# Combination stage of a hybrid Conformer/SSD layer: order of its buffers, queue of its tile loads, places of the norm's two mean products

## The chip, the cores and the metric

The kernel runs on one core of a Trainium2 chip. The core has five engines with a queue of their own each: TensorE (PE, matrix products; PEld is its weight load), VectorE (DVE), ScalarE (ACT), GpSimd (POOL) and SyncE (SP, which here only issues DMAs). An engine takes the instructions of its queue strictly in order; engines wait for one another on semaphores. Data lies in HBM; it is moved by DMA to SBUF (128 partitions) and PE writes its results to PSUM. The metric is device time in microseconds (us) of one execution, the median of several.

## What is computed

One layer over x of shape (1, 1024, 1024), all in float32: a layer norm, a token mixer with two branches, an output projection with a residual and a norm, and a convolutional gated feed-forward block. The stage that matters here joins the two branches; the layer norm of the first one goes over the 1024 channels, its convolution has 31 taps, and `ssd_branch` ends in a product from 2048 to 1024 channels:

```python
def conformer_branch(u_glu, dw_w, dw_b, ln_g, ln_b, w_out):
    a, g = jnp.split(u_glu, 2, axis=-1)
    v = a * jax.nn.sigmoid(g)
    v = causal_dwconv(v, dw_w, dw_b)
    v = jax.nn.silu(layer_norm(v, ln_g, ln_b))
    return v @ w_out

def reference(...):
    h = layer_norm(x, ln_in_g, ln_in_b)
    ...
        y_a = conformer_branch(u_glu, ...)
        y_b = ssd_branch(z, xbc, dt_raw, ...)
        mix = (jax.nn.sigmoid(gate_a) * y_a + jax.nn.sigmoid(gate_b) * y_b) @ w_o[l]
        h = layer_norm(DN_ALPHA * h + mix, ln1_g[l], ln1_b[l])
```

## The kernel before

**Tiling and stages.** The 1024 positions are worked off in two halves of 512 (hh = 0 and 1). Activations are held with channels on partitions: a 1024-channel activation is 8 tiles of 128 x 512. For each half come `mixers` (input projections, both convolutions, the SSD recurrence), `combine` (the stage changed here) and an output projection; the feed-forward block follows for all positions. A float32 product is made of three products of rounded parts, high x high, high x low and low x high (lines 170, 171, 172, in `mm3`), so `project`, one 128-column slice of a weight times 1024 channels, is 24 instructions on PE. `weights` loads a slice by SP (L145), rounds it on ACT (L147) and takes the low part on DVE (L151).

**The order of the queues.** Program order is not queue order. The framework's scheduler simulates the engines with its own durations and gives each engine, among the instructions that it holds ready, the one of highest priority. Priority is program order; `tc.high_priority(offset=n)` moves instructions n places ahead (a negative n, behind). What comes out is a fixed order for each queue; on the chip an instruction also waits for its own semaphores.

**Memory.** `mixers` and `combine` each open a pool at the same place of SBUF, one after the other. Within a pool the buffers lie in the order in which their tags first appear. `reuse_waits="tile"` means that a tile of the later pool waits on the chip only for the users of earlier tiles on its own bytes. In `mixers` the order is, in KB per partition: rstd 2, m 4, cbm 0.5, u 3 x 2, xbc 4 x 2, x4 2 x 8, zs 2 x 8, v 4 x 2.1, then smaller ones up to 84. `zs` is read last by L562, `x4` by L602 (the low parts of yT), `v` by the convolution's taps.

**The 31-tap convolution.** `conv31` runs on DVE, 30 instructions L453 for each of 8 channel tiles, two tiles at a time; it has a priority 1500 places behind, so that it fills DVE's gaps. The results of tiles 0 to 5 are stored to `c_scr` (L463); the last two (6 and 7, the dictionary `accs`) stay in SBUF.

**`combine` before.** For j in 0..7: `gate()` is a `project` of a weight gb with hT and a sigmoid on ACT (L669); the y part stored by the mixer is loaded by SP (L677); a `project` of a weight sp with yT (called sp0 to sp7 below, the gates gb0 to gb7); DVE adds and multiplies (L681, L682) into `mb` j. The gates run one ahead: gb0, gb1, sp0, gb2, sp1, and so on. Behind the loop stands the convolution's norm, raised by 900 places: SP loads the six stored tiles (L692), POOL adds the eight tiles (L697, L699), PE multiplies with a matrix of 1/1024 (**L701, the first mean product**, which gives every partition the mean over channels), DVE subtracts (L704), ACT squares (L706, L709), POOL adds the squares (L710), PE multiplies again (**L712, the second mean product**, the variance), ACT and DVE make the reciprocal root (L713, L714), and each tile is scaled (L717), goes through SiLU (L718) and is split into high and low part, sT (L186, L187). Then come eight projects co0 to co7 of the convolution's output weight with sT. In the first half `ln_in_second` reuses the buffers of this norm to make the input norm of the second half: gain and shift come into `stats` and `sq` (L276), x into `c0` to `c3` (L279).

PSUM has four banks for projects (tag `acc`) and four for the rest (tag `sm`); a project needs a free bank.

Of the kernel before, what the change touches and what calls it, by code (L numbers as in the profile page):

```python
# [8 lines left out]
F32 = mybir.dt.float32  # L9
F32R = mybir.dt.float32r  # L10
AF = mybir.ActivationFunctionType
# [5 lines left out]
P = 128  # L17
D = 1024
T = 1024
HALF = 512  # L20
# [30 lines left out]
CT_A, CT_G, CT_X, CT_B, CT_C, CT_GA, CT_GB, CT_Z = 0, 8, 16, 32, 36, 40, 48, 56  # L51
# [4 lines left out]
def kernel(  # L56
# [31 lines left out]
    def bank(which):  # L88
        n_ps[0] += 1
        pl, tag = (pacc, "acc") if which else (psm, "sm")  # L90
        return pl.tile([P, 512], F32, tag=tag, name=f"{tag}{n_ps[0]}")
# [17 lines left out]
        out=quads, in_=ident.rearrange("p (j h) -> p h j", j=4), axis=AX.X, op=ALU.add  # L109
# [23 lines left out]
    c_scr = [dram.tile([8, P, HALF], F32, name=f"c_scr{i}") for i in range(2)]  # L133
# [6 lines left out]
    y_scr = [dram.tile([8, P, HALF], F32, name=f"y_scr{i}") for i in range(2)]  # L140

    def weights(src, name, keep=None, kept=None):
        with tc.high_priority(offset=4000):
            st = wst.tile([P, D], F32, tag="st", name=f"st_{name}")
            SY.dma_start(st, src)  # L145
            w = wsp.tile([P, 2, D], F32R, tag="w", name=f"w_{name}")
            A.copy(w[:, 0, :], st)  # L147
            if kept is not None:
                SY.dma_start(w[:, 1, :].bitcast(F32), kept)
            else:  # L150
                V.tensor_tensor(  # L151
                    out=w[:, 1, :], in0=st, in1=w[:, 0, :].bitcast(F32), op=ALU.subtract
                )
            if keep is not None:
                SY.dma_start(keep, w[:, 1, :].bitcast(F32))
        return w
# [7 lines left out]
    def big_tile(name):  # L164
        return big.tile([P, 2, KD, HALF], F32R, tag="big", name=name)

    def mm3(ps, wa, xa, start, stop, more=False):


        TE.matmul(ps, wa(0), xa(0), start=start, stop=False, skip_group_check=more)  # L170
        TE.matmul(ps, wa(0), xa(1), start=False, stop=False, skip_group_check=more)  # L171
        TE.matmul(ps, wa(1), xa(0), start=False, stop=stop, skip_group_check=more)  # L172

    def project(ps, w, xs):
        for k in range(KD):
            mm3(
                ps,
                lambda i: w[:, i, k * P : (k + 1) * P],
                lambda i: xs[:, i, k, :],
                k == 0,  # L180
                k == KD - 1,
            )

    def split_to(dst, j, src):

        A.copy(dst[:, 0, j, :], src)  # L186
        V.tensor_tensor(  # L187
            out=dst[:, 1, j, :], in0=src, in1=dst[:, 0, j, :].bitcast(F32), op=ALU.subtract
        )
# [40 lines left out]
    def ln_apply(t, mv, rs, i, g, b):  # L230
        V.scalar_tensor_tensor(
            out=t, in0=t, scalar=mv[:, i, 0:1], in1=g, op0=ALU.subtract, op1=ALU.mult
        )
        V.scalar_tensor_tensor(
            out=t, in0=t, scalar=rs[:, i : i + 1], in1=b, op0=ALU.mult, op1=ALU.add
        )
# [29 lines left out]
                    transpose_to(hT, xt, t, 0, KD)  # L266
        return hT

    def ln_in_second(pl):

        hT = big_tile("hT1")
        gb = [pl.tile([P, D], F32, tag=tag, name=f"in1_{tag}") for tag in ("stats", "sq")]
        for i in range(2):
            G.dma_start(gb[i], gin[i])  # L276
        for t in range(4):
            xt = pl.tile([P, D], F32, tag=f"c{t}", name=f"x1_{t}")
            G.dma_start(xt, x[HALF + t * P : HALF + (t + 1) * P, :])  # L279
# [379 lines left out]
    def combine(hh, hT, yT, accs):  # L659

        with pool(f"comb{hh}") as pl:
            mb, gbs = [], []

            def gate():
                j = len(gbs)
                pg = bank(1)
                project(pg, weights(wcol[CT_GB + j], f"gb{hh}_{j}"), hT)
                gb = pl.tile([P, HALF], F32, tag="gate", bufs=3, name=f"gb{hh}_{j}")
                A.activation(out=gb, in_=pg, func=AF.Sigmoid)  # L669
                gbs.append(gb)  # L670

            gate()
            for j in range(8):
                if j < 7:
                    gate()
                ya = pl.tile([P, HALF], F32, tag="yb", bufs=2, name=f"yb{hh}_{j}")
                SY.dma_start(ya, y_scr[hh][j])  # L677
                ps = bank(1)
                project(ps, weights(wssm[j, 1], f"sp{hh}_{j}"), yT)
                m = pl.tile([P, HALF], F32, tag=f"mb{j}", name=f"mb{hh}_{j}")  # L680
                V.tensor_add(m, ya, ps)  # L681
                V.tensor_mul(m, m, gbs[j])  # L682
                mb.append(m)
            with tc.high_priority(offset=900):
                cs = []
                for i in range(8):
                    if i in accs:
                        cs.append(accs[i])
                        continue
                    if i % 2 == 0:  # L690
                        pair = pl.tile([P, 2, HALF], F32, tag=f"c{i // 2}", name=f"cc{hh}_{i}")
                    SY.dma_start(pair[:, i % 2, :], c_scr[hh][i])  # L692
                    cs.append(pair[:, i % 2, :])
                stats = pl.tile([P, 2, HALF], F32, tag="stats", name=f"stats{hh}")
                squares = pl.tile([P, 2, HALF], F32, tag="sq", name=f"csq{hh}")
                mean = stats[:, 0, :]
                G.tensor_add(mean, cs[0], cs[1])  # L697
                for c in cs[2:]:
                    G.tensor_add(mean, mean, c)  # L699
                pm = bank(0)  # L700
                TE.matmul(pm, mean_w, mean, start=True, stop=True)  # L701
                var = stats[:, 1, :]
                for i, c in enumerate(cs):
                    V.tensor_tensor(out=c, in0=c, in1=pm, op=ALU.subtract)  # L704
                    if i == 0:
                        A.activation(out=var, in_=c, func=AF.Square)  # L706
                    else:
                        sq = squares[:, i % 2, :]
                        A.activation(out=sq, in_=c, func=AF.Square)  # L709
                        G.tensor_add(var, var, sq)  # L710
                pv = bank(0)
                TE.matmul(pv, mean_w, var, start=True, stop=True)  # L712
                A.activation(out=var, in_=pv, func=AF.Sqrt, bias=eps)  # L713
                V.reciprocal(out=var, in_=var)  # L714
                sT = pl.tile([P, 2, KD, HALF], F32R, tag="sT", name=f"sT{hh}")
                for i, c in enumerate(cs):
                    V.tensor_mul(c, c, var)  # L717
                    A.activation(  # L718
                        out=c,
                        in_=c,  # L720
                        func=AF.Silu,
                        scale=pc[:, PC_LG + i : PC_LG + i + 1],
                        bias=pc[:, PC_LB + i : PC_LB + i + 1],
                    )
                    split_to(sT, i, c)
            mixT = big_tile(f"mixT{hh}")
# [439 lines left out]
    yT, accs = mixers(1, hT)  # L1166
    mixT, _ = combine(1, hT, yT, accs)
# [122 lines left out]
```

## Time and profile before

| | us |
|---|---|
| median of 3 runs | 1971.43 (1966.43 to 1974.03) |
| the profiled execution | 1972.21 |
| its span, first to last instruction | 1970.1 |
| PE busy | 1932.9 (98%) |
| DVE busy | 1600.7 (81%) |
| ACT busy | 1083.8 (55%) |
| POOL busy | 203.1 (10%) |

The page has the busy time of each engine, the chain of work that ended last, and groups of instructions. Views of the trace used below: the waits of PE (which line waited for which), timelines of one engine (start, duration, line, operation, output tile <- input tiles, count, and in brackets the idle time before it and what ended it), groups for one tile or one line (count, shortest/median/longest in ns, first and last start in us) and busy times in chosen windows. Consecutive like instructions are merged into one row with a count.

### The profile page before, as it was taken

Reading aid. Unit: us, or ns where it says so; the run is one execution under the profiler, and the core shown is the slowest. Engines: PE = TensorE matmul, PEld = TensorE weight load, DVE = VectorE, ACT = ScalarE, POOL = GpSimd, SP = SyncE. Lnnn points to the kernel's source line nnn. Section 1 sums busy time; section 2 is a strip of 40 time slices with the busy share of each in tenths; the row PEclk is TensorE's granted clock in tenths of the full one; section 3 lists DMA queues with packets and bytes.
Section 4 is the critical chain, followed back from the end, with each engine's and each line's share of the span. In section 5 each row is a group of like instructions: output and inputs, shape, how many; then the busy total and the mean of one; then the engine's idle time right before and its main releaser. Section 6 shows DMA issues by size and latency. Waiting matters only on the chain.

```text
span 1970.1 us, 25840 instructions
## 1 busy us (share of the span) xinstructions
PE 1932.9 (98%) x9453; PEld 1575.2 (80%) x9453; DVE 1600.7 (81%) x2224; ACT 1083.8 (55%) x1617; POOL 203.1 (10%) x246
## 2 busy tenths in 40 slices
PE   9999999999899999999999999999999999999997
PEld 8888777777688788888778888888888888878886
DVE  7599999999786547898999655587788888879778
ACT  4676767653263265868775435365555555544432
POOL 0001010110310000110101040001000000121010
PEclk9999999999999999999999999999999999999999
DMA  7645455546455665555554644576455555588673
GB/s 270 221 171 198 161 206 177 166 162 202 157 187 176 215 221 182 190 184 198 178 178 148 213 162 129 169 255 227 160 166 183 175 185 184 179 293 297 201 230 125
DMA packets 128416, 378.36 MB, mean 192 GB/s; under 512 B 15104, under 2 KB 15648, under 8 KB 128288
## 3 DMA queue, kind: packets, MB, share of 16 engines
q1 hardware_dynamic: 109152, 321.63, 48.7%
q0 software_dynamic: 12800, 43.54, 6.4%
q10 hardware_dynamic: 6336, 11.54, 1.6%
q8 instruction: 74, 1.21, 0.3%
q14 instruction: 54, 0.44, 0.1%
HBM read 289.99 MB, written 86.65 MB: 191 GB/s over the span
## 4 chain that ended last, share of the span: by engine, by line
PE 71%; DVE 16%; issue 5%; DMA 5%; ACT 2%; POOL 1%; SPq 0%; DVEq 0%; ACTq 0%; POOLq 0%
PE acc L172 16%; PE acc L171 16%; PE acc L170 16%; PE sm L171 6%; PE sm L172 6%; PE sm L170 6%; DVE c L453 5%; DVE w_c L151 1%; DVE x L408 1%; DMA rstd<-nrm_scr 1%; PE sm L536 1%; DMA dr<-wdown 1%; PE sm L539 1%; DVE x L588 1%; DMA b_scr<-fo 1%
## 5 line engine op out<-in xcount | busy, mean ns | idle before, releaser
L170 PE MATMUL acc<-hT,w_c 128*128 128x512 f32 x1000 | 391.8, 392 | 0.5 <-ACT x L406 0.5
L171 PE MATMUL acc<-hT,w_c 128*128 128x512 f32 x1000 | 390.7, 391 | 0.0
L172 PE MATMUL acc<-hT,w_c 128*128 128x512 f32 x1000 | 390.1, 391 | 0.6 <-DVE w_c L151 0.5
L453 DVE SCALAR_TENSOR_TENSOR c<-v,pc,c 128x512 f32<-128x512 f32 x480 | 370.6, 798 | 7.3 <-ACT c L442 4.7
L170 PEld LDWEIGHTS acc<-hT,w_c 128*128 128x128 f32 x1000 | 187.8, 188 | 41.7 <-issue 1.9
L172 PEld LDWEIGHTS acc<-hT,w_c 128*128 128x128 f32 x1000 | 187.8, 188 | 41.2 <-DVE w_c L151 1.4
L171 PEld LDWEIGHTS acc<-hT,w_c 128*128 128x128 f32 x1000 | 187.8, 188 | 39.2 <-issue 1.1
L147 ACT CAST w_c<-st_c 128x1024 fp32r<-128x1024 f32 x128 | 133.8, 1045 | 108.5 <-PE acc L172 90.0
L515 POOL TENSOR_TENSOR ce<-ce,xbc 128x1024 f32<-128x1024 f32 x28 | 74.1, 2648 | 694.3 <-ACT ce L514 694.3
L1077 ACT CAST w_dn<-dr 128x1024 fp32r<-128x1024 f32 (+1 forms) x73 | 68.8, 944 | 87.5 <-DMA dr<-wdown 25.3
L504 ACT ACTIVATE m<-ab,acs 128x128 f32<-128x128 f32 x256 | 78.4, 390 | 48.2 <-PE sm L536 47.0
L170 PE MATMUL sm<-h1s,w_s 128*128 128x512 f32 x264 | 102.7, 389 | 0.0
L171 PE MATMUL sm<-h1s,w_s 128*128 128x512 f32 x264 | 102.7, 389 | 0.0
L172 PE MATMUL sm<-h1s,w_s 128*128 128x512 f32 x264 | 102.2, 389 | 0.0
L151 DVE TENSOR_TENSOR w_c<-st_c,w_c 128x1024 fp32r<-128x1024 f32 x64 | 79.1, 1239 | 22.3 <-ACT w_c L147 22.1
L1078 DVE TENSOR_TENSOR w_dn<-dr,w_dn 128x1024 fp32r<-128x1024 f32 (+1 forms) x73 | 78.7, 1089 | 5.3 <-ACT w_dn L1077 5.3
L408 DVE SCALAR_TENSOR_TENSOR x<-u,pc,x 128x512 f32<-128x512 f32 x96 | 76.7, 810 | 5.7 <-ACT x L406 5.7
L172 PE MATMUL acc<-h1b,w_ue 128*128 128x512 f32 x176 | 68.9, 395 | 1.5 <-DVE w_ue L151 1.5
L170 PE MATMUL acc<-h1b,w_ue 128*128 128x512 f32 x176 | 68.8, 391 | 0.0
L171 PE MATMUL acc<-h1b,w_ue 128*128 128x512 f32 x176 | 68.6, 390 | 0.0
L170 PE MATMUL sm<-h1b,w_s 128*128 128x512 f32 x176 | 68.5, 389 | 0.0
L171 PE MATMUL sm<-h1b,w_s 128*128 128x512 f32 x176 | 68.5, 389 | 0.0
(324 smaller groups left out, 4542.3 us busy)
## 6 DMA issues: line engine op xcount, KB each, us to landing
st_c<-wcol SPq DMA_DIRECT2D x128, 512.0 KB, 4.4
low_scr<-w_c SPq DMA_DIRECT2D x64, 512.0 KB, 2.9
w_c<-low_scr SPq DMA_DIRECT2D x64, 512.0 KB, 4.4
ab<-acs_scr SPq DMA_DIRECT2D x32, 512.0 KB, 4.1
dr<-wdown SPq DMA_DIRECT2D x55, 256.0 KB, 4.8
st_wo<-wo SPq DMA_DIRECT2D x24, 512.0 KB, 4.0
st_ue<-wup SPq DMA_DIRECT2D x22, 512.0 KB, 4.2
first_scr<-first ACTq DMA_DIRECT2D x44, 256.0 KB, 2.9
```

The costliest lines, as they stand in the source:

```text
L147: A.copy(w[:, 0, :], st)
L151: V.tensor_tensor(out=w[:, 1, :], in0=st, in1=w[:, 0, :].bitcast(F32), op=ALU.subtract)
L170: TE.matmul(ps, wa(0), xa(0), start=start, stop=False, skip_group_check=more)
L171: TE.matmul(ps, wa(0), xa(1), start=False, stop=False, skip_group_check=more)
L172: TE.matmul(ps, wa(1), xa(0), start=False, stop=stop, skip_group_check=more)
L408: V.scalar_tensor_tensor(out=o, in0=u[:, k : k + HALF], scalar=pc[:, wc + k : wc + k + 1], in1=o, op0=ALU.mult, op1=ALU.add,)
L453: V.scalar_tensor_tensor(out=accs[i], in0=v[:, k : k + HALF], scalar=pc[:, wc + k : wc + k + 1], in1=accs[i], op0=ALU.mult, op1=ALU.add,)
L504: A.activation(out=m[:, h, :], in_=ab[:, h, :], func=AF.Relu, scale=-1.0, bias=acs[:, c, 8 * g + h : 8 * g + h + 1],)
L515: G.tensor_tensor(out=ce, in0=ce, in1=CT[:, cs].unsqueeze(1).to_broadcast([P, 8, P]), op=ALU.mult)
L536: TE.matmul(o, xs[:, h * HP : (h + 1) * HP], m[:, h, :], start=True, stop=first)
L1077: A.copy(w[:, 0, cs], src)
L1078: V.tensor_tensor(out=w[:, 1, cs], in0=src, in1=w[:, 0, cs].bitcast(F32), op=ALU.subtract)
```

## The change

The buffers of `combine` are named in another order: `sq` and `stats` first, then (as they come) `gate` and `yb`, then all eight `mb`, then in the first half the x tile `c3`, then `c0` to `c2`, and `sT` last. Inside j = 0, behind the y load, `early_tiles` allocates them and loads the six stored tiles by POOL's queue, raised by 5000 places; the additions of the mean stand there too, no longer raised. `deviations` (L701 to L710 of before) stands behind j = 2 in the first half and j = 1 in the second, `normed` (L712 to the splits) behind j = 4 and j = 3; before, both stood behind j = 7 and were raised by 900. `ln_in_second` takes the `c3` tile made earlier. No arithmetic is added or removed.

```diff
-    def ln_in_second(pl):
+    def ln_in_second(pl, x3):
...
-            xt = pl.tile([P, D], F32, tag=f"c{t}", name=f"x1_{t}")
+            xt = x3 if t == 3 else pl.tile([P, D], F32, tag=f"c{t}", name=f"x1_{t}")
...
+            gbs = []
+            squares = pl.tile([P, 2, HALF], F32, tag="sq", name=f"csq{hh}")
+            stats = pl.tile([P, 2, HALF], F32, tag="stats", name=f"stats{hh}")
+            late, cs = [], []
+            mean, var = stats[:, 0, :], stats[:, 1, :]
+
+            def early_tiles():
+                mb = [pl.tile([P, HALF], F32, tag=f"mb{j}", name=f"mb{hh}_{j}") for j in range(8)]
+                late.extend(
+                    pl.tile([P, D], F32, tag="c3", name=f"x1_{t}") for t in (3,) if not hh
+                )
+                pairs = [
+                    pl.tile([P, 2, HALF], F32, tag=f"c{i}", name=f"cc{hh}_{i}") for i in range(3)
+                ]
+                with tc.high_priority(offset=5000):
+                    for i in range(6):
+                        G.dma_start(pairs[i // 2][:, i % 2, :], c_scr[hh][i])
+                        cs.append(pairs[i // 2][:, i % 2, :])
+                cs.extend(accs[i] for i in (6, 7))
                 G.tensor_add(mean, cs[0], cs[1])
                 for c in cs[2:]:
                     G.tensor_add(mean, mean, c)
+                return mb
+
+            def deviations():
                 pm = bank(0)
                 TE.matmul(pm, mean_w, mean, start=True, stop=True)
...
+            def normed():
                 pv = bank(0)
                 TE.matmul(pv, mean_w, var, start=True, stop=True)
...
+            gate()
+            mb = None
+            for j in range(8):
+                if j < 7:
+                    gate()
+                ya = pl.tile([P, HALF], F32, tag="yb", bufs=2, name=f"yb{hh}_{j}")
+                SY.dma_start(ya, y_scr[hh][j])
+                if mb is None:
+                    mb = early_tiles()
+                ps = bank(1)
+                project(ps, weights(wssm[j, 1], f"sp{hh}_{j}"), yT)
+                V.tensor_add(mb[j], ya, ps)
+                V.tensor_mul(mb[j], mb[j], gbs[j])
+                if j == 2 - hh:
+                    deviations()
+                if j == 4 - hh:
+                    sT = normed()
...
-            return mixT, None if hh else ln_in_second(pl)
+            return mixT, None if hh else ln_in_second(pl, late[0])
```

More of the change, by code (lines that the diff above doesn't have):

```diff
@@ L661, in combine @@
         with pool(f"comb{hh}") as pl:
[L662 to L696, printed above, removed]
+            gbs = []
@@ L699, in combine @@
                     G.tensor_add(mean, mean, c)
+                return mb
+            def deviations():
                 pm = bank(0)
                 TE.matmul(pm, mean_w, mean, start=True, stop=True)
-                var = stats[:, 1, :]
                 for i, c in enumerate(cs):
@@ L725, in combine, with gate @@
                     split_to(sT, i, c)
+                return sT
+            def gate():
+                j = len(gbs)
+                pg = bank(1)
+                project(pg, weights(wcol[CT_GB + j], f"gb{hh}_{j}"), hT)
+                gb = pl.tile([P, HALF], F32, tag="gate", bufs=3, name=f"gb{hh}_{j}")
+                A.activation(out=gb, in_=pg, func=AF.Sigmoid)
+                gbs.append(gb)
+            gate()
[15 more added lines that the diff above has]
+                    sT = normed()
             mixT = big_tile(f"mixT{hh}")
```

## The prediction

> **What bounds the kernel now.** First the page: PE is busy through nearly the whole span, so only time in which PE stands still, or runs slowly, can be won. Then the waits of PE (total, times, longest).
>
> ```profile
> span 1970.1 us, 25840 instructions
> PE 1932.9 (98%) x9453; PEld 1575.2 (80%) x9453; DVE 1600.7 (81%) x2224; ACT 1083.8 (55%) x1617; POOL 203.1 (10%) x246
> PE sm L701 <- POOL stats L699: 5.2, 1, 5.2
> ...
> PE acc L170 <- ACT gb L669: 1.6, 1, 1.6
> ```
>
> The first of these is the longest single wait of PE in the execution: the first mean product of `combine`, in one half only. PE's timeline there:
>
> ```profile
> 519.83 0.39 PE L170 MATMUL acc<-yT,w_sp 128*128 128x512 f32 x1
> ...
> 522.32 0.39 PE L172 MATMUL acc<-yT,w_sp 128*128 128x512 f32 x1
> 527.92 2.08 PE L701 MATMUL sm<-stats,mean_w 128*128 128x512 f32 x2 [5.22 <-POOL stats L699]
> 529.01 1.42 PE L170 MATMUL acc<-yT,w_sp 128*128 128x512 f32 x1
> ...
> 531.93 0.63 PE L172 MATMUL acc<-yT,w_sp 128*128 128x512 f32 x1
> 532.36 0.63 PE L170 MATMUL acc<-hT,w_gb 128*128 128x512 f32 x1
> ...
> 534.06 0.44 PE L171 MATMUL acc<-hT,w_gb 128*128 128x512 f32 x1
> 534.34 0.39 PE L172 MATMUL acc<-hT,w_gb 128*128 128x512 f32 x1
> ```
>
> The wait is only part of the loss: behind it the products start 0.43 us apart (531.93 to 532.36), and only from 534.34 on do they run as ahead of it: 11 steps from 519.83 to 522.32, 0.227 us each, 5.44 for a project of 24. The same product in the second half waits for nothing:
>
> ```profile
> 1155.92 1.02 PE L701 MATMUL sm<-stats,mean_w 128*128 128x512 f32 x2
> 1156.38 0.79 PE L172 MATMUL acc<-hT,w_gb 128*128 128x512 f32 x1
> 1157.01 0.40 PE L170 MATMUL acc<-hT,w_gb 128*128 128x512 f32 x1
> ```
>
> L701 and one product take 1157.01 - 1155.92 = 1.09, so L701 by itself 1.09 - 0.23 = 0.86. From 522.32 to 534.34 are 12.02 us, which hold L701 and 12 products (one ahead of it, six with yT and five with hT behind it): 0.86 + 12 x 0.227 = 3.58. **The loss is 12.02 - 3.58 = 8.44 us.**
>
> Why so late? Rows of POOL (with the group of the additions in ns), SP and DVE:
>
> ```profile
> 472.91 0.57 POOL L585 DMA_DIRECT2D rstd<-nrm_scr  x1 [2.75 <-issue]
> 494.21 0.55 POOL L279 DMA_DIRECT2D x<-x  x1 [20.73 <-DMA g_scr<-gt]
> 516.76 1.28 POOL L697 TENSOR_TENSOR stats<-cc 128x512 f32<-128x512 f32 x1 [22.01 <-DMA cc<-c_scr]
> 518.29 5.71 POOL L699 TENSOR_TENSOR stats<-stats,cc 128x512 f32<-128x512 f32 x4 [0.25 <-DMA cc<-c_scr]
> 524.08 3.79 POOL L699 TENSOR_TENSOR stats<-stats,c 128x512 f32<-128x512 f32 x2
> L699 POOL TENSOR_TENSOR stats<-stats,cc x8: 1278/1297/2155, 518.3 to 1149.8; 128x512 f32<-128x512 f32 x8
> 511.63 2.98 SPq L692 DMA_DIRECT2D cc<-c_scr  x6
> 514.72 7.78 SPq L677 DMA_DIRECT2D yb<-y_scr  x4
> 511.15 1.53 DVE L453 SCALAR_TENSOR_TENSOR c<-v,pc,c 128x512 f32<-128x512 f32 x2
> 520.75 1.41 DVE L681 TENSOR_TENSOR mb<-yb,acc 128x512 f32<-128x512 f32 x2 [8.07 <-DMA yb<-y_scr]
> ```
>
> The loads go out by SP's queue at 511.63 only. The seven additions run from 516.76 to 527.87, though POOL is free from 473.5 on and six tiles lie in HBM. The last taps end at 512.68. The scheduler put L701 where by its own clock the sum was ready, and there PE stood from 522.55 on.
>
> **The change, part by part.** *Loads.* Added up in order of first use, `c0` to `c2` lay at 26 to 38 KB of the pool, over `x4` (20.5 to 36.5); now sq 4, stats 4, gate 6, yb 4, mb 16 and c3 4 go ahead, and they lie at 38 to 50, inside `zs` (36.5 to 52.5). The last readers:
>
> ```profile
> L562 DVE TENSOR_TENSOR x<-x,zs x4: 678/679/692, 405.9 to 454.9; 128x512 f32<-128x512 f32 x4
> 485.88 1.22 DVE L602 TENSOR_TENSOR yT<-x,yT 128x1024 fp32r<-128x1024 f32 x1
> ```
>
> So their bytes are free at 455.6. In POOL's queue the loads come behind the rstd load, free at 473.5: six issues of 0.55 take 3.3, cover: POOL's idle 20.73. If the x tile's load (into `c3`, over `x4`, free at 487.1) stands between loads and additions, these start at 487. Five additions at 1.28 to 2.16 end by 498 at the latest. Nothing else waits in POOL's queue, so a wait there holds up nobody. SP loses six issues: the first y load goes out at 511.6, not 514.7, which ends DVE's 8.07 earlier; PE did not wait for it, so I count nothing.
>
> *Additions beside the taps.* Taps beside a POOL operation appear in these rows:
>
> ```profile
> 431.66 2.83 POOL L515 TENSOR_TENSOR ce<-ce,xbc 128x1024 f32<-128x1024 f32 x1 [12.29 <-ACT ce L514]
> 432.15 3.54 DVE L453 SCALAR_TENSOR_TENSOR c<-v,pc,c 128x512 f32<-128x512 f32 x2
> ```
>
> Two taps, 1.53 by themselves (511.15 above), took 3.54: 2.01 lost in 2.83 us of POOL, 0.71 of it. Five additions at 1.28 then delay the taps by 5 x 1.28 x 0.71 = 4.5 us (bounds: 0, and 5 x 2.16 = 10.8, every addition as long as the longest of the group row and DVE standing throughout). I take 4.5, since the row is of this very pair: the taps end at 517.2. Two more additions, 1.28 to 2.16 each: sum ready at 519.8 to 521.5; at the upper bound 512.7 + 10.8 + 4.3 = 527.8. [...]
>
> *First mean product.* No longer raised, it comes behind sp2. Six products of sp2 were left at 522.55, so sp2 ends at 523.9 with PE at full rate: 2 us or more behind the sum. Wait and slow stretch go: **-8.44**. [...] The rows show 0.43 us steps for 6 us behind the wait, so 8.44 stays.
>
> *Second mean product and what follows.* It moves behind sp4: 523.9 + 0.86 + 4 x 5.44 = 546.5. Needed by then: the sum of squares.
>
> ```profile
> 541.08 4.76 POOL L710 TENSOR_TENSOR stats<-stats,csq 128x512 f32<-128x512 f32 x3 [0.21 <-ACT csq L709]
> 549.33 1.02 PE L712 MATMUL sm<-stats,mean_w 128*128 128x512 f32 x2
> 572.68 1.27 DVE L187 TENSOR_TENSOR sT<-c,sT 128x512 fp32r<-128x512 f32 x2
> L170 PE MATMUL acc<-sT,w_co x64: 389/389/389, 578.1 to 625.9; 128*128 128x512 f32 x64
> 580.00:600.00 20.00, 20.00 (x90) 16.57 (x89) 20.00 (x29) 5.12 (x8) 2.14 (x4) 1.00 0.67 224
> ```
>
> Before it came 545.84 - 530.0 = 15.8 after L701; now at 540.6, 5.9 ahead. From L712 to the last split of sT are 24.6 us, so sT is whole at 571.1. PE reaches co0 at 578.1 - 8.44 = 569.7 at the earliest and needs the last eighth 4.8 later, at 574.5: 3.4 to spare. Cost 0.
>
> *Second half.* L701 moves from 1155.92 to the end of sp1, 4 + 24 products later (about 1162.3), L712 to about 1185 (behind sp3). The sum was ready at 1155.9 already, and nothing makes it later:
>
> ```profile
> 1160.37 11.61 POOL L710 TENSOR_TENSOR stats<-stats,csq 128x512 f32<-128x512 f32 x7 [6.22 <-ACT csq L709]
> L681 DVE TENSOR_TENSOR mb<-yb,acc x16: 668/684/689, 520.7 to 1224.1; 128x512 f32<-128x512 f32 x16
> ```
>
> Squares by 1172.0 + 7 = 1179, sT by 1185 + 24.6 = 1210, co0 behind sp7 at 1223. Nothing won, nothing lost.
>
> *The 1.6 us wait for L669 stays.* The first gate sigmoids stand late in ACT's queue, as the y and c loads do in SP's. I read this so: the scheduler hands out work on the new pool's tiles only when, by its own clock, the old pool's last user is through, here the taps. The change leaves that as it is, so 0; if the sigmoids came earlier, -1.6.
>
> **Sum.** 0 + 0 - 8.44 + 0 + 0 = -8.44 in the profiled execution: span 1970.1 to 1961.7, with the 2.1 us around it 1972.2 to 1963.8. It stands 0.8 above the median 1971.43; from the median, **1963.0 us** (-0.43%).
>
> **Rivals.** *The additions slow the taps so far that the sum is late.* For it: the 3.54 us row. At the upper bound the sum comes at 527.8, L701 waits 3.9, and if PE slows again as behind the 5.22 (8.44 - 5.37 = 3.1 more) 7.0 of the 8.44 are given back: 1964 to 1970. Against it: that bound takes all five additions at their longest and DVE as wholly stopped, where the row has 0.71.
>
> *The early work does not come early*, since POOL's queue keeps it behind something that ends with the taps. Then seven additions end at about 527.9 as before, and the place 1.3 us later saves that alone, plus 0 to 3 if the y loads are out of their way: 1967 to 1970, no change to speak of. For it: the loads waited in both halves until the mixers' last user was done. Against it: that order was SP's; POOL's has nothing in between but the x load at 494.
>
> *sT becomes late for co0, slower than before.* The variance product at its fixed place is only 2.8 us earlier while PE is 8.4 earlier, and DVE is full (20.00 of 20 in the window row). It decides from 8.7 us of delay of sT: 3.4 to spare, then 5.3 of idle that, with 3.1 of slow products, eats up 8.4. At 12 us of delay: 8.6 + 3.1 - 8.4 = +3.3, 1975. For it: the split of sT shares DVE with weights, `mb` and the input norm. Against it: only one of four x tiles can be ahead of sT in DVE's queue (its statistics and two passes).
>
> **How the numbers follow.** Forecast 0.66, slowed taps 0.14, not early 0.11, sT late 0.09. The scheduler orders all queues anew behind the change, and other PE waits (single ones up to 1.6, so two of them) can come or go, some 3 us either way; the three runs shown lie within 1966.43 to 1974.03, 0.2% about their median. Lower end: 8.44 + 1.6 + 3 = 13.0 won, 1958.4, and 1.4 more for the spread of a measurement: 1957. Upper end: the first two rivals, 1970.5. About 0.5%, 9.9 us, is what a measurement can tell from no change. Faster by more needs the 1.6 or a lucky order as well: 0.32. Within: 0.61. Slower by over 0.5%, 1981, is only sT very late or an order gone wrong: 0.07.
>
> **What would show it.** Right: no PE wait at L701 in either half, no 0.43 us steps at 520 to 535, POOL's loads at 473 to 490 and five additions before 500, taps stretched wherever POOL adds and over at 515 to 520, the squares' sum ahead of L712. Wrong: additions still behind 512 (second rival), a wait at L701 of 1 to 4 us with the sum ready behind 523 (first), a wait of PE for sT or for DVE's splits at co0 (third), or new waits elsewhere of several us from the new order.

## The result, and the profile after

| | us |
|---|---|
| before, median of 10 runs | 1970.27 (1966.43 to 1974.03) |
| after, median of 10 runs | 1963.51 (1960.09 to 1968.60) |
| ratio after to before | 0.9969, 95% interval 0.9957 to 0.9981 |
| the profiled execution after | 1962.23, span 1960.5 |

The change wins 0.31%, 3.7 to 8.5 us by the interval. The forecast was 1963.0. First two lines of the page of the changed kernel (its span, and the busy time of each engine), then its waits of PE (total, times, longest):

```profile
span 1960.5 us, 25846 instructions
PE 1928.3 (98%) x9453; PEld 1572.2 (80%) x9453; DVE 1599.4 (82%) x2224; ACT 1083.5 (55%) x1617; POOL 216.8 (11%) x258
```

```profile
PE sm L536 <- DVE m L531: 3.3, 3, 1.4
...
PE acc L172 <- DVE w_gb L151: 1.8, 2, 1.4
...
PE acc L170 <- ACT gb L721: 1.6, 1, 1.6
...
PE acc L172 <- DVE w_sp L151: 0.9, 1, 0.9
```

The 5.2 us wait for the sum is gone (the first mean product is L688 now). In its place stand a larger wait for the low part of `w_gb` (0.6 before) and one for that of `w_sp` (none before); the wait for the gate sigmoid (L721 now) is as it was. PE's timeline around the first mean product, which stands 12 products into gb4:

```profile
530.29 0.40 PE L172 MATMUL acc<-hT,w_gb 128*128 128x512 f32 x1
530.52 1.02 PE L688 MATMUL sm<-stats,mean_w 128*128 128x512 f32 x2
530.98 0.79 PE L170 MATMUL acc<-hT,w_gb 128*128 128x512 f32 x1
531.61 0.40 PE L171 MATMUL acc<-hT,w_gb 128*128 128x512 f32 x1
531.84 0.39 PE L172 MATMUL acc<-hT,w_gb 128*128 128x512 f32 x1
```

There is no idle time ahead of it, and from the second product behind it on the steps are 0.23 us. A window of the kernel before, then of the kernel after (bounds, length, busy time of PE, PEld, DVE, ACT, POOL, then the granted clock of PE, the DMA share and GB/s):

```profile
500.00:530.00 30.00, 23.15 (x95) 17.85 (x94) 20.60 (x22) 6.29 (x8) 10.47 (x7) 0.96 0.47 160
```

```profile
500.00:530.00 30.00, 27.96 (x122) 22.53 (x121) 26.72 (x35) 7.33 (x9) 2.94 (x2) 1.00 0.39 129
```

PE's idle time falls from 6.85 to 2.04, and the clock, 0.96 here before (and 0.93 from 530 to 560), is 1.00 in both stretches. Why the sum is early enough, in POOL's timeline of the changed kernel:

```profile
474.31 0.57 POOL L585 DMA_DIRECT2D rstd<-nrm_scr  x1 [3.15 <-issue]
474.87 3.23 POOL L678 DMA_DIRECT2D cc<-c_scr  x6
489.40 0.55 POOL L279 DMA_DIRECT2D x<-x  x1 [11.30 <-DVE yT L602]
489.97 2.09 POOL L681 TENSOR_TENSOR stats<-cc 128x512 f32<-128x512 f32 x1
492.14 7.23 POOL L683 TENSOR_TENSOR stats<-stats,cc 128x512 f32<-128x512 f32 x4
510.29 1.65 POOL L683 TENSOR_TENSOR stats<-stats,c 128x512 f32<-128x512 f32 x1 [10.91 <-DVE c L453]
520.95 1.29 POOL L683 TENSOR_TENSOR stats<-stats,c 128x512 f32<-128x512 f32 x1 [9.02 <-DVE c L453]
```

The six loads leave at 474.87 instead of 511.63, five additions are over at 499.4, and the sum is ready at 522.2 instead of 527.87.

**Where the time went.** To compare executions I take one stretch of the first half, called **the stage** below: from the first high x high product with a gate weight to the last one with the convolution's output weight. It holds the same products of PE in every kernel (578 in the trace, in either half). It is read from the groups by tile (count, shortest/median/longest ns, first and last start); before, its first start was

```profile
L170 PE MATMUL acc<-hT,w_gb x64: 389/389/632, 483.0 to 571.5; 128*128 128x512 f32 x64
```

and its last 625.9 (shown in the prediction): 142.9 us. After:

```profile
L170 PE MATMUL acc<-hT,w_gb x64: 389/389/793, 484.2 to 567.0; 128*128 128x512 f32 x64
...
L170 PE MATMUL acc<-sT,w_co x64: 389/389/389, 578.5 to 621.4; 128*128 128x512 f32 x64
```

621.4 - 484.2 = 137.2: **5.7 us won in the stage**. The same stretch of the second half has no wait of PE and takes 131.6 in both kernels. The rest of the 9.6 us by which the two spans differ lies outside the stage: ahead of the stage +1.2, between the two stages 509.2 to 505.8, behind the second 703.4 to 701.7. In the other twelve profiles, before included, all with the same work there, these two stretches took 505.7 to 512.0 and 702.1 to 708.0, so I take that part for scatter, and the L536 waits above (6.5 before) for a part of it: in a second profile of the changed kernel the stretch between took 509.0, and these waits made 6.3.

Of the 8.44 us forecast, then, 2.7 were given back inside the stage. PE's timeline of the changed kernel, only the rows with idle time ahead:

```profile
486.23 0.50 PE L172 MATMUL acc<-hT,w_gb 128*128 128x512 f32 x1 [1.41 <-DVE w_gb L151]
...
498.28 0.50 PE L172 MATMUL acc<-yT,w_sp 128*128 128x512 f32 x1 [0.87 <-DVE w_sp L151]
...
504.42 0.50 PE L172 MATMUL acc<-hT,w_gb 128*128 128x512 f32 x1 [0.41 <-DVE w_gb L151]
...
511.34 0.50 PE L170 MATMUL acc<-yT,w_sp 128*128 128x512 f32 x1 [1.63 <-ACT gb L721]
```

These four waits make 4.32 us; 131.6 + 4.32 = 135.9, so 1.3 is left, 0.3 for each wait. About half of this lies in how idle time is counted: it starts at the recorded end of the product before, 0.39 behind that product's start, where without a wait the next one would have started 0.23 behind it (0.16). Most of the rest is the first product behind a wait, which takes longer (0.50 in these rows) and is followed 0.34 later, not 0.23 (0.11). Before, the stage had waits of 0.57, 1.63 and 5.22. The account "131.6, plus each wait, plus 0.3 for each" is tested on all kernels below.

**Theory** after the result: the gain comes from the loads being early, through POOL's queue; the fixed places and the order of the buffers are not needed for it; and the 2.7 us come from POOL's additions beside the taps, which delay the weights' low parts in DVE's queue. **Rivals**: the places carry the gain; the order carries it; the new waits come from the scheduler's new order of the queues and not from the additions.

### The profile page after: what moved, and what is told of

It is laid out like the page before. It is cut to its first block, busy times and chain, and to the rows that moved or that the text cites. A ratio compares the mean times of both kernels' runs of the same rounds, so it can differ in the third digit from the quotient of the medians.

```text
span 1960.5 us, 25846 instructions
## 1 busy us (share of the span) xinstructions
PE 1928.3 (98%) x9453; PEld 1572.2 (80%) x9453; DVE 1599.4 (82%) x2224; ACT 1083.5 (55%) x1617; POOL 216.8 (11%) x258
## 3 DMA queue, kind: packets, MB, share of 16 engines
q8 instruction: 74, 1.21, 0.2%
## 4 chain that ended last, share of the span: by engine, by line
PE 57%; DVE 10%; DMA 5%; ACT 2%; issue 2%; SPq 0%; DVEq 0%; ACTq 0%
PE acc L172 13%; PE acc L171 13%; PE acc L170 13%; PE sm L171 5%; PE sm L172 5%; PE sm L170 5%; DVE c L453 3%; DMA dr<-wdown 1%; DMA dr<-b_scr 1%; DVE w_dn L1093 1%; DMA b_scr<-fo 1%; DVE x L408 1%; PE sm L536 1%; DVE rows L231 1%; DVE rows L234 1%
## 5 line engine op out<-in xcount | busy, mean ns | idle before, releaser
L147 ACT CAST w_c<-st_c 128x1024 fp32r<-128x1024 f32 x128 | 133.8, 1045 | 108.9 <-PE acc L172 82.3
L515 POOL TENSOR_TENSOR ce<-ce,xbc 128x1024 f32<-128x1024 f32 x28 | 80.1, 2861 | 678.6 <-ACT ce L514 678.6
## 6 DMA issues: line engine op xcount, KB each, us to landing
st_c<-wcol SPq DMA_DIRECT2D x128, 512.0 KB, 4.4
low_scr<-w_c SPq DMA_DIRECT2D x64, 512.0 KB, 2.9
w_c<-low_scr SPq DMA_DIRECT2D x64, 512.0 KB, 4.4
ab<-acs_scr SPq DMA_DIRECT2D x32, 512.0 KB, 4.1
st_wo<-wo SPq DMA_DIRECT2D x24, 512.0 KB, 4.1
st_ue<-wup SPq DMA_DIRECT2D x22, 512.0 KB, 3.9
```

Source lines behind the costliest of these rows:

```text
L515: G.tensor_tensor(out=ce, in0=ce, in1=CT[:, cs].unsqueeze(1).to_broadcast([P, 8, P]), op=ALU.mult)
```

## The experiments

### Loads in SP's queue again

```diff
-                        G.dma_start(pairs[i // 2][:, i % 2, :], c_scr[hh][i])
+                        SY.dma_start(pairs[i // 2][:, i % 2, :], c_scr[hh][i])
```

> The changed kernel with its six tile loads in SP's queue again; order of the buffers and places of the two mean products stay. Theory (the early loads carry the gain): the loads leave SP at about 512 only, behind the last taps, the seven additions end at about 527.9 as in the kernel before, the first mean product stands behind sp2, due at about 524, waits some 4 us there and has slow products behind it; the taps are not stretched and end at about 513. Of the 8.4 us only 1 to 2 are won: median 1967 to 1970. Rival (the fixed places carry the gain): the first mean product waits less than 1 us, median 1961 to 1964.

Measured: 1968.96 (1964.77 to 1972.90), ratio 0.9987 (0.9975 to 0.9998); stage 139.8. PE's timeline of this kernel at the first mean product:

```profile
527.16 2.07 PE L688 MATMUL sm<-stats,mean_w 128*128 128x512 f32 x2 [3.74 <-POOL stats L683]
528.25 1.42 PE L170 MATMUL acc<-hT,w_gb 128*128 128x512 f32 x1
...
529.89 0.58 PE L172 MATMUL acc<-hT,w_gb 128*128 128x512 f32 x1
530.30 0.39 PE L170 MATMUL acc<-hT,w_gb 128*128 128x512 f32 x1
```

The product waits 3.74 us at its fixed place. With late loads 0.13% of time is won, where the changed kernel won 0.31%: the theory's case. But in the stage 3.1 of the 5.7 us stay, more than the 1 to 2 that I expected: at its later place the product waits 3.74 instead of 5.22, the slow products behind it end sooner (3.1 us behind the start of the first instead of 6.4), and neither the `w_sp` wait nor the larger first `w_gb` wait is there (0.42). So with late loads the new place (or the order of the buffers, which this run does not tell from it) is worth something.

### Places undone

```diff
-                if j == 2 - hh:
-                    deviations()
-                if j == 4 - hh:
-                    sT = normed()
+            with tc.high_priority(offset=900):
+                deviations()
+                sT = normed()
```

> The changed kernel with the two mean products and what hangs on them written behind j = 7 again, raised by 900; early loads and the order of the buffers stay. Theory (early loads carry it): sum ready at about 522 as in the changed kernel, no wait of PE for it, median 1962 to 1965, not to be told from the changed kernel. Rival (the fixed places carry it): the raised product stands ahead of its sum and PE waits 2 us or more there, median 1967 or more.

Measured: 1965.50 (1963.77 to 1968.84), half a microsecond above the expected span, ratio 0.9976 (0.9966 to 0.9987); stage 137.0. No wait at the first mean product; the waits are 1.29, 0.88, 0.40 and 1.63, those of the changed kernel. With early loads the places are worth nothing that shows.

### The queue alone

To the kernel before:

```diff
-                    SY.dma_start(pair[:, i % 2, :], c_scr[hh][i])
+                    with tc.high_priority(offset=5000):
+                        G.dma_start(pair[:, i % 2, :], c_scr[hh][i])
```

> The kernel before with one edit: its six tile loads go through POOL's queue, raised by 5000 places. Order of the buffers and places of the mean products are those of before. Theory (early loads carry it): the loads wait for the readers of x4, since the tiles lie over x4 here, and leave at about 487 instead of 475; five additions are over by about 501, sum ready at about 522, no wait of PE for it, median 1962 to 1965. Rival (order and places are needed): the loads or the additions come behind 512, or PE still waits 2 us or more at the first mean product, median 1967 to 1971.

Measured: 1964.22 (1961.91 to 1969.05), ratio 0.9974 (0.9964 to 0.9984); stage **134.5**, 8.4 less than before. POOL's timeline of this kernel, then PE's (rows with idle time, and the first mean product, L702 here):

```profile
486.41 3.24 POOL L693 DMA_DIRECT2D cc<-c_scr  x6 [13.88 <-DVE yT L602]
498.99 3.42 POOL L698 TENSOR_TENSOR stats<-cc 128x512 f32<-128x512 f32 x1
```

```profile
506.82 0.50 PE L170 MATMUL acc<-yT,w_sp 128*128 128x512 f32 x1 [1.63 <-ACT gb L669]
524.60 0.50 PE L172 MATMUL acc<-hT,w_gb 128*128 128x512 f32 x1 [0.67 <-DVE w_gb L151]
527.01 1.02 PE L702 MATMUL sm<-stats,mean_w 128*128 128x512 f32 x2
```

Two lines of the whole change do its work, and in the stage better than all of it: the loads wait for L602 as expected, 11.5 us later than in the changed kernel, and this is early enough. The five additions are over at 509.2, not at 501 as I expected, and the sum is ready at 519.1, ahead of the expected 522; PE does not wait for it. That the median is not lower than the changed kernel's, although its stage is 2.7 shorter, lies within the scatter of the other stretches; by its interval it won 3.2 to 7.1, less than the 8.4 of its stage, and why stays open.

### All additions behind the taps

```diff
-                G.tensor_add(mean, cs[0], cs[1])
-                for c in cs[2:]:
+                G.tensor_add(mean, cs[6], cs[7])
+                for c in cs[:6]:
```

> The changed kernel with the mean summed in another order, tiles 6 and 7 first, so that all seven additions stand behind the last taps; loads, places and order of the buffers stay. Theory on what was given back (additions beside the taps delay the weights' low parts, and PE waits for those): taps end at about 513.7 instead of 520.8, PE waits for the low parts of w_gb and w_sp fall from 1.8 and 0.9 to about 0.6 together, the sum is ready at 523 to 525 and the product at about 528 does not wait; median 1960.5 to 1962.5, 1 to 3 below the changed kernel. Rival (the waits for low parts come from the new order of the queues alone): these waits stay at 2 us or more in total, median 1963 to 1965. Other rival: seven late additions are too late, PE waits 1 us or more for the sum, median 1964 to 1967.

Measured: 1963.95 (1961.02 to 1964.40), ratio 0.9961 (0.9949 to 0.9973); stage 135.3, and a median above the expected 1960.5 to 1962.5. The taps end at 513.6, the sum is ready at 526.1, later than expected, and the product does not wait. The `w_sp` wait and the second `w_gb` wait are gone; but against the expectation the first `w_gb` wait stays:

```profile
485.12 0.50 PE L172 MATMUL acc<-hT,w_gb 128*128 128x512 f32 x1 [1.42 <-DVE w_gb L151]
```

At 485 no addition runs in this kernel or in the changed one. So this wait has another cause, and my theory that the additions cause all of it fell. What stands ahead of that low part in DVE's queue are the products with the rstd tile (L588), which wait for its load. DVE's row of the kernel before, then of the changed kernel:

```profile
478.96 2.74 DVE L588 SCALAR_TENSOR_TENSOR x<-x,pc,rstd 128x512 f32<-128x512 f32 x4 [3.34 <-DMA rstd<-nrm_scr]
```

```profile
480.97 2.74 DVE L588 SCALAR_TENSOR_TENSOR x<-x,pc,rstd 128x512 f32<-128x512 f32 x4 [4.36 <-DMA rstd<-nrm_scr]
```

From the issue of the rstd load (472.91 and 474.31) that is 6.05 and 6.66. In the changed kernel the six loads go out right behind it. Over all thirteen profiles: 5.69 to 6.23 where they don't (six kernels), 6.66 to 7.30 where they do (seven). **The early loads hold up the rstd tile by 0.9 us** (means 6.02 and 6.90).

### The old order of the buffers

```diff
-            squares = pl.tile([P, 2, HALF], F32, tag="sq", name=f"csq{hh}")
-            stats = pl.tile([P, 2, HALF], F32, tag="stats", name=f"stats{hh}")
...
                 pairs = [
                     pl.tile([P, 2, HALF], F32, tag=f"c{i}", name=f"cc{hh}_{i}") for i in range(3)
                 ]
+                stats = pl.tile([P, 2, HALF], F32, tag="stats", name=f"stats{hh}")
+                two.append(stats)
+                two.append(pl.tile([P, 2, HALF], F32, tag="sq", name=f"csq{hh}"))
```

(and `c3` is allocated in `ln_in_second` again.)

> The changed kernel with the buffers of the kernel before in their old order (gate, yb, mb, c, stats, sq, sT, c3); POOL's queue for the loads and the fixed places stay. Measured by the stage: from the first product of a gate weight (line 170) to the last product of the convolution's output weight (line 170) in the first half, 142.9 us before, 137.2 changed, 134.5 with the queue alone. Theory (the new order lets the additions start some 10 us earlier, right where the low parts of w_gb and w_sp are due, and gives 2 to 3 us back): loads leave at about 487, additions start at about 499, PE's waits for the low parts of w_gb and w_sp fall from 2.7 to under 1 in total, the stage takes 134.5 to 135.5. Rival (the give-back comes from the fixed places or from something else that e8 lacked): the stage stays at 136.5 to 137.5. Median 1962 to 1965 in either case, since the other stages scatter by more.

Measured: 1965.28 (1961.56 to 1968.19), ratio 0.9977 (0.9967 to 0.9986); stage 136.0, between the two expectations. The loads leave at 487.49, the additions start at 500.67. The first `w_gb` wait falls to 0.82 and the `w_sp` wait is gone, but a new one of 1.01 stands at gb4 (525.66; in "queue alone" it is the 0.67 at 524.60). The additions now lengthen the taps from 502 on (four take 6.85 us from 502.26, where four take 2.74 with all additions behind them), and they end at 518.8; the y loads leave SP at 517.79 only (512.61 in the kernel with all additions behind the taps), and gb4's low part stands in DVE's queue behind the `mb` rows that wait for the first of them:

```profile
521.59 0.69 DVE L736 TENSOR_TENSOR mb<-yb,acc 128x512 f32<-128x512 f32 x1 [2.83 <-DMA yb<-y_scr]
...
524.39 1.22 DVE L151 TENSOR_TENSOR w_gb<-st_gb,w_gb 128x1024 fp32r<-128x1024 f32 x1
```

With additions beside the taps a low part comes late in either order of the buffers; the order sets which one.

### Twice the additions beside the taps

```diff
+                for i in range(1, 6):
+                    G.tensor_add(squares[:, 0, :], cs[i - 1], cs[i])
                 G.tensor_add(mean, cs[0], cs[1])
```

> The changed kernel with five more POOL additions of the same shape (two tiles in, a scratch tile out) among the first five, beside the taps. Theory (additions beside the taps delay the taps and the weights' low parts, and PE waits for these): the last tap ends 4 to 8 us later than in the changed kernel (520.8), so at 525 to 529, the sum is ready at 526 to 531, PE's waits for low parts of w_gb and w_sp grow from 2.7 to 4 or more, and the stage takes 139 us or more against 137.2. Rival (the additions cost PE nothing, the waits come from the order of the queues): the taps end within 2 us of 520.8 or the low parts' waits stay within 1 us of 2.7, stage 136.5 to 138.

Measured: 1974.75 (1970.88 to 1980.58), ratio 1.0024 (1.0010 to 1.0038), slower than before; stage 144.8. DVE's timeline of this kernel (taps and low parts), then PE's:

```profile
488.82 5.17 DVE L453 SCALAR_TENSOR_TENSOR c<-v,pc,c 128x512 f32<-128x512 f32 x3
493.92 2.31 DVE L151 TENSOR_TENSOR w_sp<-st_sp,w_sp 128x1024 fp32r<-128x1024 f32 x1
496.14 10.20 DVE L453 SCALAR_TENSOR_TENSOR c<-v,pc,c 128x512 f32<-128x512 f32 x6
```

```profile
507.53 0.80 PE L172 MATMUL acc<-hT,w_gb 128*128 128x512 f32 x1 [5.48 <-DVE w_gb L151]
508.12 0.63 PE L170 MATMUL acc<-hT,w_gb 128*128 128x512 f32 x1
```

Six taps take 10.20 instead of 5.09, the low part behind them is 5.48 late, and PE falls into the slow steps again (0.43 us each, from 508.12 on). The last tap ends at 523.9, a little earlier than I expected; the waits and the stage are as the theory has them. The price of the additions is paid by the weights queued behind the taps.

### The first gate tile outside the stage's pool

```diff
-                gb = pl.tile([P, HALF], F32, tag="gate", bufs=3, name=f"gb{hh}_{j}")
+                if j:
+                    gb = pl.tile([P, HALF], F32, tag="gate", bufs=3, name=f"gb{hh}_{j}")
+                else:
+                    gb = statep.tile([P, HALF], F32, tag="g0", name=f"gb{hh}_{j}")
```

> The changed kernel with the first gate tile of each half in the pool of the states instead of the stage's own, so that its sigmoid need not stand behind the users of the old pool. Theory (the 1.6 us wait of PE for the gate sigmoid comes from the scheduler handing out work on the new pool's tiles only when the old pool's last user is through): the first sigmoid stands ahead of two weight roundings in ACT's queue, PE's wait for it of 1.6 goes or shrinks to under 0.5, and the stage takes about 135.6 against 137.2, median 1960 to 1963. Rival (PE runs into the next late thing, the second sigmoid or the low parts, at once): the waits before sp2's end stay at 4 us in total, stage 136.5 to 137.5.

Measured: stage 135.3, as expected; 1965.51 (1960.44 to 1969.65), ratio 0.9972 (0.9961 to 0.9983), above the expected time, and not to be told from the changed kernel. ACT's timeline of the changed kernel, then of this one:

```profile
509.74 1.04 ACT L147 CAST w_sp<-st_sp 128x1024 fp32r<-128x1024 f32 x1 [5.09 <-PE acc L172]
510.69 1.57 ACT L721 ACTIVATE gb<-acc 128x512 f32<-128x512 f32 x3
```

```profile
491.94 0.59 ACT L724 ACTIVATE gb<-acc 128x512 f32<-128x512 f32 x1
```

Three sigmoids stood behind a weight rounding that itself waited for PE to give a weight buffer back. With its tile elsewhere the first one runs some 18 us earlier, and PE's wait for it is gone; nothing takes its place. So the wait comes from that tile's lying in the stage's pool; by which rule the scheduler then puts the sigmoid so late was not tried.

### The queue and the gate tile

The two edits "queue alone" and "gate tile" on the kernel before.

> The kernel before with two edits only: the six loads in POOL's queue, raised by 5000, and the first gate tile of each half in the pool of the states. Theory: the queue alone gave 134.5 us for the stage, the gate's wait of 1.6 goes as well: 132.9, against the 131.6 that the second half takes in every kernel so far; median 1959 to 1963, the fastest so far. Rival (the wait moves to the second sigmoid or to the low parts): 134 to 135, median 1962 to 1965.

Measured: 1962.68 (1959.02 to 1963.80), ratio 0.9962 (0.9948 to 0.9975); stage 133.6, 0.7 above the expected value, with waits of 0.52, 0.15 and 0.33: the gate's wait is gone, and three short ones for low parts are left.

### All three causes removed, and controls

Additions behind the taps, old order of the buffers, and the gate tile, on the changed kernel:

> The changed kernel with three edits together: the mean summed from tiles 6 and 7 on (no addition beside the taps), the buffers in the old order (loads at about 487 instead of 474, so not right behind the rstd load), the first gate tile in the pool of the states. Theory (the stage is 131.6 us, as in the second half, plus every wait of PE in it, each of which costs its idle time and some 0.28 more): left is only the first w_gb wait of about 0.6, no w_sp wait, no gate wait, so 132.4 to 133.0 against 137.2 of the changed kernel; median 1959 to 1963. Rival (the waits are made up by others as soon as they go): stage 134 or more.

The same with the new order of the buffers:

> As the previous kernel, but with the new order of the buffers, so that the six loads leave right behind the rstd load at about 474. Theory (the loads make the rstd tile land about 0.75 us later, DVE's row of it starts 6.8 instead of 6.1 us after the issue, and the first w_gb low part comes later by as much): the wait for the first w_gb low part is 1.3 to 1.5 instead of 0.6, and the stage takes 133.2 to 133.8. Rival (the order is worth nothing once the additions are out of the way): the same as the previous kernel within 0.3.

The changed kernel again:

> The changed kernel itself once more, beside the two others: stage 137.2, waits of PE in it of 1.4, 0.9, 0.4 and 1.6 as in its first profile, median 1962 to 1966. If these waits scatter from run to run, the accounts of the other kernels by single waits fall.

Measured: 1961.08 (1956.49 to 1962.42), ratio **0.9946** (0.9935 to 0.9958), stage 132.4, for the first; 1965.45 (1961.83 to 1966.52), ratio 0.9967 (0.9956 to 0.9979), stage 133.8, for the second; 1964.72 (1963.70 to 1965.76), ratio 0.9967 (0.9955 to 0.9978), stage 136.9, for the changed kernel. The only row of the first kernel's stage in which PE has idle time ahead, and the same of the second:

```profile
483.85 0.50 PE L172 MATMUL acc<-hT,w_gb 128*128 128x512 f32 x1 [0.45 <-DVE w_gb L151]
```

```profile
484.95 0.50 PE L172 MATMUL acc<-hT,w_gb 128*128 128x512 f32 x1 [1.86 <-DVE w_gb L151]
```

The order of the buffers alone makes the difference, 1.41 of wait and 1.4 of stage; from the rstd load's issue to DVE's row it is 5.69 in the first and 7.30 in the second, the extremes of all profiles, so this pair shows more than the mean of 0.9 (and a longer wait than the 1.3 to 1.5 expected). By its median the first is the fastest kernel of all, 0.54% ahead of the kernel before. In the changed kernel the four waits come back as 1.17, 0.87, 0.41 and 1.63: they do not scatter much. All kernels in one table (the account is 131.6 + waits + 0.3 for each wait):

| kernel | waits of PE in the stage | account | stage | median |
|---|---|---|---|---|
| before | 0.57, 1.63, 5.22 | 139.9 | 142.9 | 1970.27 |
| changed | 1.41, 0.87, 0.41, 1.63 | 137.1 | 137.2 | 1963.51 |
| changed, again | 1.17, 0.87, 0.41, 1.63 | 136.9 | 136.9 | 1964.72 |
| loads by SP | 0.42, 1.63, 3.74 | 138.3 | 139.8 | 1968.96 |
| places undone | 1.29, 0.88, 0.40, 1.63 | 137.0 | 137.0 | 1965.50 |
| queue alone | 1.63, 0.67 | 134.5 | 134.5 | 1964.22 |
| late additions | 1.42, 1.63 | 135.3 | 135.3 | 1963.95 |
| old order | 0.82, 1.63, 1.01 | 136.0 | 136.0 | 1965.28 |
| additions doubled | 1.22, 0.86, 5.48, 1.63 | 142.0 | 144.8 | 1974.75 |
| gate tile | 1.45, 0.88, 0.41 | 135.2 | 135.3 | 1965.51 |
| queue, gate tile | 0.52, 0.15, 0.33 | 133.5 | 133.6 | 1962.68 |
| late, gate tile | 1.86 | 133.8 | 133.8 | 1965.45 |
| late, gate tile, old order | 0.45 | 132.4 | 132.4 | 1961.08 |

The account holds to 0.1 in the ten profiles with no wait above 2 us; in the other three it lacks 1.5 to 3.0, the slow products behind the long wait. Waits and stage are read from one profile of each kernel. The medians follow the stages only within some 3 us (the median less the stage is 1826.3 to 1831.7), since the other stretches scatter.

## Why the prediction was right, and what it mis-sized

- **Bound and mechanism: right.** The wait of 5.22 and the slow steps are gone, and the loads' queue did it, as the rows of POOL and SP said. The place of the product, to which the working gave a part of its own, was not needed: with early loads the sum was ahead of the product wherever the scheduler put it (places undone, queue alone).
- **The time: 1963.0 against 1963.51, in part by luck.** The medians of ten runs differ by 6.8, where 8.4 was forecast; the forecast started from a median of three runs that stood 1.2 above that of ten, and this made up most of the difference. The wait with its slow products was sized right: 142.9 - 131.6, less the other two waits of before (0.57 and 1.63) with 0.3 each, leaves 8.5. But the sum was too large for the stage: -5.7, and -6.0 in the second profile.
- **The step that failed is the cost 0 beside the additions and the loads.** "Nothing else waits in POOL's queue, so a wait there holds up nobody" is true of the queue and passes over the transfers: the six loads, which the new order of the buffers lets go out right behind the rstd load, hold up the rstd tile by 0.9 us in the mean of all profiles, and the first `w_gb` wait grows from 0.57 to 1.41 (+0.84). In this pair of profiles 0.6 of it is this delay (6.05 to 6.66); the rstd load itself also left later behind the store ahead of it in POOL's queue (L584; 3.75 instead of 3.35, a distance that is 3.35 to 3.75 over all kernels, whichever queue and order they have). Over all profiles this wait is 1.40 in the mean where the loads follow at once and 0.46 where they don't.
- **The delay of the taps was about right in size, in part by luck, and priced at the wrong place.** Rows of DVE before, then after:

```profile
488.81 2.07 DVE L453 SCALAR_TENSOR_TENSOR c<-v,pc,c 128x512 f32<-128x512 f32 x3
490.80 1.21 DVE L151 TENSOR_TENSOR w_sp<-st_sp,w_sp 128x1024 fp32r<-128x1024 f32 x1
491.94 4.06 DVE L453 SCALAR_TENSOR_TENSOR c<-v,pc,c 128x512 f32<-128x512 f32 x6
```

```profile
490.82 5.17 DVE L453 SCALAR_TENSOR_TENSOR c<-v,pc,c 128x512 f32<-128x512 f32 x3
495.91 2.31 DVE L151 TENSOR_TENSOR w_sp<-st_sp,w_sp 128x1024 fp32r<-128x1024 f32 x1
498.14 5.09 DVE L453 SCALAR_TENSOR_TENSOR c<-v,pc,c 128x512 f32<-128x512 f32 x6
```

3.10 + 1.10 + 1.03 = 5.2 us, against 4.5. Two errors of the working offset each other there. It took the additions at 1.28 each, 6.4 for five, and they took 2.09 + 7.23 = 9.3, since they are slowed as well; and its share of 0.71 divides by the whole POOL row, which began ahead of the taps (they share 2.34 us, from 432.15 to 434.49, so 0.86), where here DVE lost 5.2 in 9.3, 0.56. I followed this delay to the taps' end and the sum, which had room, and not to the low parts between the taps, which had less: `w_sp` +0.87 and `w_gb` +0.41, with 0.3 each 1.9. That and the 0.84 are the 2.7 given back (8.44 - 2.7 = 5.7). Not only the taps are slowed: in the rows above the subtraction for a low part takes 2.31 us beside a POOL addition, 1.21 without one.
- **Taps' end and sum.** 520.8 instead of 517.2: DVE's row behind the rstd load starts 2.0 later in this profile (480.97 against 478.96), the five additions cost 0.7 more than forecast, and the 0.9 that is left I put down to the addition at 510.29, which runs beside one more group of taps. The sum at 522.2 is 0.7 past the forecast's 521.5, and still early: sp2 ends at about 527.8, not 523.9.
- **What follows.** The second mean product stood at 550.4 (forecast 546.5), behind the squares' sum of 545.4; sT was whole at 574.9 (571.1), and PE did not wait for it: co0 starts at 578.5, since the scheduler now put all of sp7 ahead of it. The rival "sT late" is out.
- **Second half: right.** 131.6 before and after.
- **The gate's wait: right.** It stayed, and it comes from the place of the gate's tile, as the gate tile run shows: 1.6 us, 1.9 with the 0.3. The scheduler's rule that the working read into it is not shown.
- **The rivals.** "Slowed taps" had the right mechanism and the wrong victim: with twice the additions it is the whole result (+0.24%). "Not early" is what the loads by SP do. In the changed kernel neither came true.

## What to carry to other kernels

When work is moved beside an engine that it slows, follow the delay to every instruction queued behind on that engine, not only to the chain that the move is for: here six taps took 5.09 us instead of 4.06, and the first victim was a weight's low part with no slack. A transfer issued early, because its memory happens to be free, can hold up the urgent one ahead of it (0.9 us here); here early enough was better than earliest. Where a kernel is bound by one engine, take the same stretch of its work in every profile and add up the waits in it: here the waits accounted for that stretch to 0.1 us, where medians of whole runs followed it only to some 3.

## What the runs showed of the hardware that was not expected

- **A wait costs PE 0.3 us beyond the idle time that the profile gives it**, for waits of 0.15 to 1.86 us alike (table); 0.16 of this is the way idle time is counted, as said above.
- **The slow stretch behind a long wait is a stretch of half clock, of 3.4 or 6.8 us in the three kernels that have one.** From the first product behind the wait to the first step of 0.23 us it takes 6.4 us after 5.22 of idle time (527.92 to 534.34), 3.1 after 3.74 (527.16 to 530.30 above) and 6.1 after 5.48 (507.53 to 513.60, a row of the same timeline); in the stage there is none after 1.9 or less (behind the 1.86 the steps are 0.24 and 0.23 from the second product on). The granted clock (the third figure from the end) in a window of the kernel before, then of the one with the loads by SP:

```profile
527.35:534.10 6.75, 6.18 (x13) 4.22 (x14) 5.66 (x8) 2.13 (x4) 0.52 (x1) 0.50 0.33 113
```

```profile
526.90:530.20 3.30, 3.04 (x5) 1.81 (x6) 3.27 (x5) 0.05 (x1) 0.21 (x1) 0.50 0.32 92
```

It is 1.00 up to 527.30 and from 534.20 on, and up to 526.85 and from 530.30 on; with the additions doubled it is 0.50 from 506.70 to 513.45 and 1.00 up to 506.65 and from 513.50 on (0.89 in the mean from 500 to 530). So half clock lasts 6.8, 3.4 and 6.8 us, and it sets in while PE still waits: some 0.6, 0.3 and 0.8 us ahead of the first product. What sets these lengths is not shown.
- **Where six loads of 256 KB are issued right behind a small one on the same queue, DVE's row that waits for the small one starts 0.9 us later** (6.90 instead of 6.02 us behind its issue, means of seven and six profiles). Whether they compete in the queue's own work or in the DMA engines was not tried.
